# Local attention in a hybrid mixer step: four subtractions and two sums of the softmax by GpSimd, the scale of the values in ScalarE's copy

## The chip, the cores and the metric

The kernel runs on one core of a Trainium2 chip. The metric is device time in microseconds (us) of one execution. The core's engines each work through a list of their own, in order: TensorE (PE in the rows, PEld its weight loads), VectorE (DVE), ScalarE (ACT), GpSimd (POOL), and SyncE (SP), which here issues nearly all DMAs. They wait for one another by semaphores. An instruction that waits holds up everything behind it on its engine.

## The reference, cut to what matters

Two layers. In each, 2048 latent tokens (16 tiles of 128) and 128 context tokens (one tile) go through one input projection, three groups of heads (a state-space scan, gated linear attention, windowed attention) and one output projection. The change is in the windowed attention: four query heads in two key groups, 64 wide, 128 queries against up to four blocks of 128 keys, with a learned sink logit per head in the softmax and a gate on the result.

```python
qh = rms_norm(aq, q_norm); kh = rms_norm(ak, k_norm)      # per head, then rotary
s = einsum('bnqkgd,bnskd->bnkgqs', qb, k_win) * scale     # masked band, and context keys
p = softmax(concatenate([sink, s_ctx, s_loc], axis=-1))
o = einsum(p_ctx, v_ctx) + einsum(p_loc, v_win)
y_att = o * silu(ag)
```

## The kernel before

Everything is computed in float32 accuracy out of pairs of float16 numbers, an upper and a lower part: a product is three float16 matmuls (upper by lower, lower by upper, upper by upper), which is why PE has so many of them.

Each layer has a stage for attention, from about 336 to 600 us of the span in the first layer and from about 1476 to 1740 us in the second. It is a software pipeline over the 17 tiles. For a latent tile t the loop calls, in this order, `att_project` of a tile some way ahead, `att_weights` of tile t + 2, `att_values` of tile t, and `gla_out` of tile t - 1 (the end of the linear attention, which has nothing to do with the change but shares all engines). Loads of weights for the next stage (L246 to L268) lie among them.

`att_project` multiplies a tile with the weights of queries, keys and values (L281 on PE), copies queries and keys to the tile `qkx`, of which there is a single buffer (L788, L789 on ACT), squares them (L793 on GpSimd), sums the squares and adds a constant (L795, L796 on VectorE), takes the power -1/2 (L186 on GpSimd, written to `ars`), multiplies by that and by the weights of the norm (L799, L800 on VectorE), forms the rotary product (two L817 on GpSimd, L818 and L819 on VectorE), and splits the result into upper parts (L823, L722 on ACT) and lower parts (L824, L723 on VectorE). A DMA turns the parts around for PE (L828).

`att_weights` multiplies queries and keys of four heads to scores in PSUM (L854, L856), takes each head's maximum (four L857 on VectorE) and makes the negative shift `nm` of the exponential from it (L861, L864). `sd` is the sink's term: a sum of 128x4 numbers (L865, VectorE) and its exponential (L866, ACT). Then for each of the four heads: the exponential with its row sum (L872, ACT), the upper half of it (L874, ACT), the lower half, which is a subtraction of 128x512 numbers (L875: for the first head on VectorE, for the other three on GpSimd), and a DMA that turns both around (L876). At the end the row sums and the sink's term are added (L877, VectorE, 128x4), inverted (L879, VectorE), and multiplied by a scale `igv` of the values (L880, VectorE) to `rl`.

`att_values` multiplies the values with the weights (L892), copies the result out of PSUM (L895, ACT), transposes it (L898), makes the gate (L903 on ACT, L904 on VectorE), multiplies the gate by `rl` (L905, GpSimd) and both together (L907, VectorE).

The tiles `pr` and `p16`, which L872, L874 and L875 write, have two buffers each. The order of the instructions on each engine isn't that of the code: a scheduler goes over the whole program when it is built and sets it by its own estimate of costs, so an edit in one place can move instructions in others.

Of the kernel before, what the change touches and what calls it, by code (L numbers as in the profile page):

```python
# [14 lines left out]
AF = mybir.ActivationFunctionType  # L15
ALU = mybir.AluOpType
# [62 lines left out]
def hybrid_kernel(ctx, tc, a, o):  # L79
    nc = tc.nc  # L80
    V, S, G, T, D = nc.vector, nc.scalar, nc.gpsimd, nc.tensor, nc.sync
# [44 lines left out]
    def sb(tag, shape, dt=F32):  # L126
        if tag not in where:
            return small.tile(shape, dt, tag=tag, name=tag, bufs=1 if tag in ONCE else 2)
        ph, off, words, n = where[tag]
        off += words * rot(range(n), tag)  # L130
        return view(home.get(ph, work)[:, off:off + words], shape, dt)
# [699 lines left out]
    def att_blocks(s, t):  # L831
        if t == CT:
            return [(s.kt[t], s.v[t], None)]
        blocks = [(s.kct, s.vc, None)]
        if t > 0:
            blocks.append((s.kt[t - 1], s.v[t - 1], 0))
        blocks.append((s.kt[t], s.v[t], None))
        if t < NT - 1:
            blocks.append((s.kt[t + 1], s.v[t + 1], 1))
        return blocks  # L840

    def att_weights(l, s, t):

        blocks = att_blocks(s, t)
        nb = len(blocks)
        mx = sb("mx", [P, 4])
        sc = []
        for hh in range(4):
            kv, gg = hh // 2, hh % 2
            ps = psum(None, "s")  # L850
            for b, (kt, _, mk) in enumerate(blocks):
                bs = slice(b * P, (b + 1) * P)
                for j in range(2):
                    T.matmul(ps[:, bs], lhsT=s.qt[t][:, 2 * gg + kv], rhs=kt[:, 2 * kv + j], start=(j == 0), stop=(j == 1 and mk is None))  # L854
                if mk is not None:
                    T.matmul(ps[:, bs], lhsT=ident_b, rhs=amask[:, mk], start=False, stop=True)  # L856
            V.tensor_reduce(mx[:, hh:hh + 1], ps[:, :nb * P], AX.X, ALU.max)  # L857
            sc.append(ps)
            yield
        nm = sb("nm", [P, 4])  # L860
        V.scalar_tensor_tensor(nm, mx, s.isc[:, 0:1], s.sink, ALU.mult, ALU.max)  # L861

        sd = sb("sd", [P, 4])
        V.tensor_scalar(nm, nm, -1.0, 14.0 * math.log(2.0), ALU.mult, ALU.add)  # L864
        V.tensor_tensor(sd, s.sink, nm, ALU.add)  # L865
        S.activation(sd, sd, AF.Exp)  # L866
        ls = sb("ls", [P, 4])
        s.pt[t] = [view(x, [P, 2 * nb, 2, P], F16) for x in rot(s.pts, "pts")]
        for hh in range(4):
            kv, gg = hh // 2, hh % 2  # L870
            pr = sb("pr", [P, 512])[:, :nb * P]
            S.activation(pr, sc[hh][:, :nb * P], AF.Exp, scale=s.isc[:, 0:1], bias=nm[:, hh:hh + 1], accum_out=ls[:, hh:hh + 1])  # L872
            p16 = sb("p16", [P, 2, nb * P], F16)
            S.copy(p16[:, 0], pr)  # L874
            (G if hh else V).tensor_tensor(p16[:, 1], pr, p16[:, 0], ALU.subtract)  # L875
            D.dma_start_transpose(out=s.pt[t][kv][:, :, gg], in_=p16.rearrange("p j c -> p (j c)"))  # L876
        V.tensor_tensor(ls, ls, sd, ALU.add)  # L877
        s.rl[t] = rot(k_rl, "rl")
        V.reciprocal(s.rl[t], ls)  # L879
        V.tensor_scalar(s.rl[t], s.rl[t], s.igv, None, ALU.mult)  # L880

    def att_values(l, s, t):
        blocks = att_blocks(s, t)
# [2 lines left out]
        po = psum()  # L886
# [5 lines left out]
                    T.matmul(po[ks, 0:256], lhsT=blocks[b][1][:, vi, ks], rhs=pts[kv][:, pj * nb + b].rearrange("p g s -> p (g s)"), start=(n == 0), stop=(n == 3 * nb - 1))  # L892
                n += 1
        ot = sb("aoy", [P, 2, P])
        S.copy(ot, po[:, 0:256].rearrange("p (g s) -> p g s", g=2))  # L895
        py = psum()
        for gg in range(2):
            T.transpose(py[:, gg * P:(gg + 1) * P], ot[:, gg], ident)  # L898
# [561 lines left out]
```

## Time and profile before

| what | us |
|---|---|
| median of three runs | 2352.64 (2347.4 to 2353.36) |
| the profiled execution | 2334.53 |
| its span, first to last instruction | 2332.8 |
| PE busy | 2089.6 (90%) |
| VectorE busy | 1628.6 (70%) |
| ScalarE busy | 991.8 (43%) |
| GpSimd busy | 872.7 (37%) |

The profiled execution lies 18 us (0.8%) under the median of the runs and 1.7 us over its own span. A share of the whole span says little here: the stages differ, and a change in the attention stages is read from their own stretches. In a timeline row, the figure in brackets is the idle time of the engine before the instruction, and what ended it.

### The profile page before, as it was taken

How to read it: one execution, taken by the hardware profiler on the slowest of the kernel's cores; microseconds unless marked ns; L12 is line 12 of the kernel's file. 1: busy time of each engine (PE TensorE's matmuls, PEld its weight loads, DVE VectorE, ACT ScalarE, POOL GpSimd, SP SyncE). 2: the span in 40 equal slices, each digit the busy share in tenths (PEclk: the TensorE clock that was granted, in tenths of full speed). 3: DMA queues.
4: the chain of work that ended last, by engine and by line, in shares of the span. 5: the costliest groups of instructions: out<-in, count | busy, mean ns of one | idle time of the engine just before them, and what ended most of it. 6: DMA issues, size and time to landing. Idle time of an engine off the chain costs nothing. (4 is left out here: it accounts for less than half of the span.)

```text
span 2332.8 us, 53735 instructions
## 1 busy us (share of the span) xinstructions
PE 2089.6 (90%) x21245; PEld 1735.9 (74%) x21245; DVE 1628.6 (70%) x4088; ACT 991.8 (43%) x2183; POOL 872.7 (37%) x906
## 2 busy tenths in 40 slices
PE   3688958899899999899999995888999999999998
PEld 0455747778787788788888884777878778878887
DVE  2566767887789888865564656777788988864442
ACT  2443545555445334433333643555563533422221
POOL 0010014566443444544431001456643344454442
PEclk6798979999999999999999997999999999999999
DMA  8697433567611013577656123456671101265643
GB/s 294 182 256 188 108 85 87 119 150 166 135 56 37 33 42 124 164 188 177 170 151 174 42 75 93 93 110 149 154 153 55 37 32 42 78 171 167 163 141 98
DMA packets 486353, 288.02 MB, mean 123 GB/s; under 512 B 354344, under 2 KB 447924, under 8 KB 483796
## 3 DMA queue, kind: packets, MB, share of 16 engines
q1 hardware_dynamic: 483796, 271.99, 44.5%
q0 software_dynamic: 2304, 12.58, 1.6%
q8 instruction: 167, 2.74, 0.5%
q14 instruction: 86, 0.70, 0.1%
HBM read 141.11 MB, written 64.93 MB: 88 GB/s over the span
## 5 line engine op out<-in xcount | busy, mean ns | idle before, releaser
L281 PEld LDWEIGHTS <-HT 128*128 128x128 f16 x6528 | 585.3, 100 | 170.8 <-issue 93.0
L281 PE MATMUL pd<-slot,HT 128*128 128x256 f16 x3456 | 432.1, 278 | 50.0 <-ACT work L806 29.7
L281 PEld LDWEIGHTS <-slot 128*128 128x128 f16 x4320 | 394.3, 97 | 105.9 <-issue 41.2
L281 PE MATMUL pd<-slot,work 128*128 128x256 f16 x3264 | 365.5, 273 | 2.1 <-DMA work<-work 2.1
L281 PEld LDWEIGHTS <-work 128*128 128x128 f16 x3264 | 319.2, 98 | 42.6 <-DMA work<-work 2.6
L281 PE MATMUL pd<-HT,slot 128*128 128x260 f16 (+3 forms) x2592 | 316.5, 269 | 13.2 <-DMA HT<-work 12.4
L281 PE MATMUL ps<-HT,slot 128*128 128x260 f16 (+1 forms) x1728 | 201.5, 270 | 4.5 <-DVE work L1054 4.5
L281 PE MATMUL ps<-slot,HT 128*128 128x256 f16 x1440 | 175.6, 281 | 19.1 <-ACT work L1188 14.3
L1248 POOL TENSOR_TENSOR work<-work 128x512 f32<-128x512 f32 x68 | 89.2, 1312 | 185.5 <-DVE work L1247 176.3
L875 POOL TENSOR_TENSOR work<-work 128x512 f16<-128x512 f32 (+2 forms) x102 | 117.4, 1154 | 85.1 <-ACT work L874 70.3
L1054 DVE SCALAR_TENSOR_TENSOR work<-ps,work 128x256 f32<-128x256 f32 (+1 forms) x288 | 134.0, 465 | 11.9 <-ACT work L1052 7.6
L1054 DVE SCALAR_TENSOR_TENSOR work<-pd,work 128x256 f32<-128x256 f32 (+1 forms) x288 | 132.5, 464 | 3.7 <-ACT work L1052 0.9
L872 ACT ACTIVATE work<-ps,nm,K 128x512 f32<-128x512 f32 (+2 forms) x136 | 100.9, 744 | 73.1 <-DVE nm L864 58.3
L1116 POOL TENSOR_TENSOR work<-work 128x512 f32<-128x512 f32 x68 | 73.2, 1081 | 113.3 <-ACT work L1074 61.8
L1056 ACT ACTIVATE work<-work 128x256 f32<-128x256 f32 (+1 forms) x144 | 58.1, 403 | 121.0 <-DVE work L1054 82.8
L1088 POOL TENSOR_TENSOR work<-K,work 128x512 bf16<-128x512 bf16 x68 | 72.2, 1063 | 77.9 <-PE ps L1100 77.2
L281 PE MATMUL pm<-slot,HT 128*128 128x256 f16 x816 | 98.8, 277 | 1.6 <-DVE work L907 1.5
L854 PEld LDWEIGHTS <-work 128*128 128x128 f16 x1008 | 74.4, 98 | 34.7 <-issue 31.9
L874 ACT CAST work<-work 128x512 f16<-128x512 f32 (+2 forms) x136 | 78.1, 589 | 46.2 <-DMA slot<-work 26.3
L669 POOL MEMSET work<- 128x512 f32 x2 | 1.1, 525 | 256.2 <-PE pm L616 256.2
L1057 DVE SCALAR_TENSOR_TENSOR work<-work 128x256 f32<-128x256 f32 (+1 forms) x144 | 81.9, 569 | 19.1 <-ACT work L1056 18.0
L1214 ACT ACTIVATE work<-work 128x512 bf16<-128x512 f32 x68 | 42.7, 629 | 119.2 <-DMA work<-work 53.6
(374 smaller groups left out, 4035.1 us busy)
## 6 DMA issues: line engine op xcount, KB each, us to landing
slot<-in_w_in_dram SPq DMA_DIRECT2D x24, 1024.0 KB
ymix<-work SPq DMA_DIRECT2D x68, 128.0 KB
yacc<-work SPq DMA_DIRECT2D x34, 256.0 KB
work<-ymix SPq DMA_DIRECT2D x34, 256.0 KB
work<-yacc SPq DMA_DIRECT2D x34, 256.0 KB
x<-work SPq DMA_DIRECT2D x17, 512.0 KB
work<-x SPq DMA_DIRECT2D x17, 512.0 KB
out_dram<-work SPq DMA_DIRECT2D x17, 512.0 KB
```

The costliest lines, as they stand in the source:

```text
L281: T.matmul(out, lhsT=lhs(i, k), rhs=rhs(j, k), start=(n == 0), stop=(n == 3 * KB - 1))
L854: T.matmul(ps[:, bs], lhsT=s.qt[t][:, 2 * gg + kv], rhs=kt[:, 2 * kv + j], start=(j == 0), stop=(j == 1 and mk is None))
L872: S.activation(pr, sc[hh][:, :nb * P], AF.Exp, scale=s.isc[:, 0:1], bias=nm[:, hh:hh + 1], accum_out=ls[:, hh:hh + 1])
L874: S.copy(p16[:, 0], pr)
L875: (G if hh else V).tensor_tensor(p16[:, 1], pr, p16[:, 0], ALU.subtract)
L1054: V.scalar_tensor_tensor(acc[:, jj, :W], pp[:, q:q + W], s.cw[j][:, q, jj:jj + 1], acc[:, jj, :W], ALU.mult, ALU.add)
L1056: S.activation(th[:, :W], acc[:, jj, :W], AF.Tanh)
L1057: V.scalar_tensor_tensor(acc[:, jj, :W], th[:, :W], 1.0, acc[:, jj, :W], ALU.add, ALU.mult)
L1088: G.tensor_tensor(sr[:, j:j + 4], oh[:, j:j + 4].unsqueeze(2).to_broadcast([P, 4, P]), at.unsqueeze(1).to_broadcast([P, 4, P]), ALU.mult)
L1116: G.tensor_tensor(xw, x, bc8(s.wst[:, t, 8 * d:8 * d + 8]), ALU.mult)
L1214: S.activation(junk, ym[:, 512 * i:512 * i + 512], AF.Square, accum_out=ss[:, i:i + 1])
L1248: G.tensor_tensor(xs[:, js], xs[:, js], tm, ALU.add)
```

## The change

`sd` (L865) and the sum before the reciprocal (L877) go from VectorE to GpSimd. The subtraction L875 goes to GpSimd for all four heads; before, it was three of four. The multiplication by `igv` (L880) is left out, and ScalarE's copy of the values out of PSUM (L895) applies that scale instead. With 17 tiles in each of two layers, that is 34 times each.

```diff
-        V.tensor_tensor(sd, s.sink, nm, ALU.add)
+        G.tensor_tensor(sd, s.sink, nm, ALU.add)
...
-            (G if hh else V).tensor_tensor(p16[:, 1], pr, p16[:, 0], ALU.subtract)
+            G.tensor_tensor(p16[:, 1], pr, p16[:, 0], ALU.subtract)
...
-        V.tensor_tensor(ls, ls, sd, ALU.add)
+        G.tensor_tensor(ls, ls, sd, ALU.add)
         s.rl[t] = rot(k_rl, "rl")
         V.reciprocal(s.rl[t], ls)
-        V.tensor_scalar(s.rl[t], s.rl[t], s.igv, None, ALU.mult)
...
-        S.copy(ot, po[:, 0:256].rearrange("p (g s) -> p g s", g=2))
+        S.activation(ot, po[:, 0:256].rearrange("p (g s) -> p g s", g=2), AF.Copy, scale=s.igv)
```

VectorE loses 136 instructions, GpSimd gains 102, ScalarE keeps its number but for two more loads of its function table in the second layer's `ssd_decays`. Lines after L880 have a number lower by one in the changed kernel (L905 is L904 there).

The scheduler sets a new order through both attention stages and the ones that follow. On GpSimd, in the second layer, between the square of tile 10's queries and keys (L793) and the power of its sums (L186 with `ars`), this stands before:

```order
L875 TENSOR_TENSOR work<-work 128x512
L793 TENSOR_TENSOR work<-work 128x384
L875 TENSOR_TENSOR work<-work 128x512
L186 TENSOR_TENSOR ars<-avar,K 128x6
L875 TENSOR_TENSOR work<-work 128x512
L186 TENSOR_TENSOR grs<-gvar,K 128x4
L817 TENSOR_TENSOR work<-work 128x12x16 x2
```

In the changed kernel the same tile on the same engine reads:

```order
L875 TENSOR_TENSOR work<-work 128x512 x2
L793 TENSOR_TENSOR work<-work 128x384
L877 TENSOR_TENSOR ls<-ls,sd 128x4
L875 TENSOR_TENSOR work<-work 128x512
L186 TENSOR_TENSOR ars<-avar,K 128x6
L875 TENSOR_TENSOR work<-work 128x512
L186 TENSOR_TENSOR grs<-gvar,K 128x4
```

The sum L877 now stands between the two, ahead of a subtraction; it does so in 17 of 34 tiles.

On VectorE, in the second layer, tile 9, from the shift of the exponential to the lower parts of the queries and keys (L824, L723), this stands before:

```order
L864 TENSOR_SCALAR nm<-nm 128x4
L865 TENSOR_TENSOR sd<-K,nm 128x4
L904 SCALAR_TENSOR_TENSOR work<-work,pd 128x256
L818 TENSOR_TENSOR work<-work 128x384
L819 TENSOR_TENSOR work<-work 128x384
L875 TENSOR_TENSOR work<-work 128x512
L824 TENSOR_TENSOR work<-work 128x4x64
L723 TENSOR_TENSOR work<-work 128x2x128
```

In the changed kernel it is (L903 is the former L904):

```order
L864 TENSOR_SCALAR nm<-nm 128x4
L903 SCALAR_TENSOR_TENSOR work<-work,pd 128x256
L818 TENSOR_TENSOR work<-work 128x384
L819 TENSOR_TENSOR work<-work 128x384
L824 TENSOR_TENSOR work<-work 128x4x64
L723 TENSOR_TENSOR work<-work 128x2x128
```

The two rows that went to GpSimd are gone, and L824 follows L819 directly.

## Rows read from the trace of the kernel before

**Rows 1.** Busy time by stretch, both attention stages; columns in the first line.

```profile
core 0: us, PE busy (x) PEld busy (x) DVE busy (x) ACT busy (x) POOL busy (x), PEclk, DMA share, GB/s
336.00:600.00 264.00, 235.94 (x2509) 202.06 (x2506) 200.14 (x475) 148.61 (x361) 149.21 (x163) 0.98 0.59 128
...
1476.00:1740.00 264.00, 236.98 (x2582) 202.02 (x2582) 204.72 (x514) 148.99 (x360) 152.05 (x166) 0.97 0.64 139
```

**Rows 2.** Timeline, 1644.9 to 1660.8, one turn of `qkx`: start, duration, engine.

```profile
1644.99 0.47 ACT L788 ACTIVATE work<-pd,waqi 128x256 f32<-128x256 f32 x1 [0.23 <-DVE work L824]
...
1645.87 0.83 POOL L793 TENSOR_TENSOR work<-work 128x384 f32<-128x384 f32 x1 [1.25 <-ACT work L789]
...
1646.86 0.54 DVE L795 TENSOR_REDUCE avar<-work 128x6 f32<-128x384 f32 x1
...
1649.42 1.32 POOL L186 TENSOR_TENSOR ars<-avar,K 128x6 f32<-128x6 f32 x1
...
1653.95 0.55 DVE L800 TENSOR_TENSOR work<-work,K 128x384 f32<-128x384 f32 x1
...
1654.63 1.15 POOL L817 TENSOR_TENSOR work<-work 128x192 f32<-128x192 f32 x2 [1.80 <-issue]
...
1655.84 0.53 DVE L865 TENSOR_TENSOR sd<-K,nm 128x4 f32<-128x4 f32 x1
...
1656.87 0.96 DVE L819 TENSOR_TENSOR work<-work 128x384 f32<-128x384 f32 x1
...
1658.16 0.69 DVE L875 TENSOR_TENSOR work<-work 128x512 f16<-128x512 f32 x1 [0.33 <-ACT work L874]
1658.55 0.41 ACT L823 CAST work<-work 128x256 f16<-128x256 f32 x1
1658.73 1.16 POOL L875 TENSOR_TENSOR work<-work 128x512 f16<-128x512 f32 x1 [1.31 <-ACT work L874]
...
1658.99 1.18 DVE L824 TENSOR_TENSOR work<-work 128x256 f16<-128x256 f32 x1
...
1660.28 0.47 ACT L788 ACTIVATE work<-pd,waqi 128x256 f32<-128x256 f32 x1 [0.25 <-DVE work L824]
```

**Rows 3.** Groups by shape, VectorE: count, busy us, mean ns, idle before.

```profile
L875 DVE TENSOR_TENSOR work<-work 128x512 f16<-128x512 f32 x28 | 24.4, 870 | 8.4 <-ACT work L874 7.8 <-DMA work<-gen 0.5
...
L880 DVE TENSOR_SCALAR K<-K 128x4 f32<-128x4 f32 x34 | 12.2, 359 | 0.5
...
L877 DVE TENSOR_TENSOR ls<-ls,sd 128x4 f32<-128x4 f32 x34 | 9.0, 265 | 6.7 <-ACT work L872 6.6
L865 DVE TENSOR_TENSOR sd<-K,nm 128x4 f32<-128x4 f32 x34 | 8.8, 260 | 0.7
```

**Rows 4.** The same for GpSimd.

```profile
L875 POOL TENSOR_TENSOR work<-work 128x512 f16<-128x512 f32 x84 | 101.9, 1217 | 63.3 <-ACT work L874 48.8 <-issue 12.1 <-DVE K L879 0.9
...
L186 POOL TENSOR_TENSOR grs<-gvar,K 128x4 f32<-128x4 f32 x34 | 37.1, 1091 | 40.8 <-DVE gvar L698 39.7 <-DVE K L879 0.8
...
L875 POOL TENSOR_TENSOR work<-work 128x128 f16<-128x128 f32 x6 | 2.6, 442 | 10.3 <-ACT work L874 10.3
```

**Rows 5.** Line L864, VectorE: ns min/median/max.

```profile
L864 DVE TENSOR_SCALAR nm<-nm x34: 154/170/689, 338.2 to 1713.7; 128x4 f32<-128x4 f32 x34
```

**Rows 6.** Line L879, VectorE, the same columns.

```profile
L879 DVE RECIPROCAL K<-ls x34: 160/172/179, 344.7 to 1724.9; 128x4 f32<-128x4 f32 x34
```

**Rows 7.** Groups by shape, ScalarE: the exponential, the copy of the values, a table load.

```profile
L872 ACT ACTIVATE work<-ps,nm,K 128x512 f32<-128x512 f32 x112 | 86.6, 776 | 46.6 <-DVE nm L864 34.5 <-DVE work L875 7.5 <-POOL work L875 4.1
...
L895 ACT COPY work<-pm 128x256 f32<-128x256 f32 x34 | 12.8, 376 | 9.1 <-PE pm L892 9.1
...
L943 ACT ACT_TABLE_LOAD x2 | 2.6, 1283 | 0.0
```

**Rows 8.** Timeline of VectorE, 1625 to 1629, another turn of `qkx`.

```profile
1625.98 1.65 DVE L875 TENSOR_TENSOR work<-work 128x512 f16<-128x512 f32 x1
...
1627.88 0.41 DVE L824 TENSOR_TENSOR work<-work 128x256 f16<-128x256 f32 x1
```

## The prediction

> **What bounds the kernel now.** I read the busy time by stretch first, because the change touches only the two attention stages [rows 1]. Each is 264 us long, PE is busy for 236 and 237 of them, VectorE for 200 and 205, GpSimd for 149 and 152, ScalarE for 149. No engine is full, so these stages are set by waits between engines. What the stages can give at most is PE's idle time in them, 28 and 27 us, together 55 us. PE has the same matmuls to do after the change.
>
> Which waits? I followed one buffer through the timeline. The tile `qkx` exists once, so L788 can write the next tile's queries only when L824 has read the last ones. One turn is in [rows 2]: from L788 at 1644.99 to the next L788 at 1660.28, which starts 0.11 us after L824 ends (1658.99 + 1.18) and is marked as waiting for it. The turn takes 15.3 us and crosses GpSimd three times (L793, L186, L817), VectorE six times (L795, L796, L799, L800, L818 with L819, L824) and ScalarE in between. I read all 32 latent turns of the two layers in the same way: the mean from L788 to the last read is 15.3 us, and only 0.6 us more pass until the next L788. So this buffer's chain is close to the period of the stage. About 9 us of a turn are the instructions themselves. The rest is queueing: the chain's next instruction has its data, and its engine is doing something else. Summed over 32 turns that is 122 us on VectorE, 43 us on GpSimd, 26 us on ScalarE. The price of the change is what it does to these three numbers. After [rows 1] the other stages keep their work.
>
> **The change part by part.** *VectorE loses four instructions per tile.* By their busy time that is 24.4 + 12.2 + 9.0 + 8.8 = 54 us [rows 3]; this is the upper end, as if all of it lay on the path, and the lower end is 0. In the 32 turns I counted how much of each removed instruction runs while an instruction of the chain waits behind it: L875 11.2 us, L877 2.9, L865 2.0, L880 0.6, together **17 us**. [rows 8] shows the largest piece: L875 takes 1.65 us, and L824 comes only after it. In [rows 2] it is part of L865, ahead of L818 and L819. I take 17 us as the gain. The waits that go with these instructions cost VectorE another 8.4 and 6.7 us of idle time ahead of L875 and L877 [rows 3], hardly any of it ahead of the chain, so I add nothing.
>
> *GpSimd gains 34 subtractions and 68 sums of 128x4.* A subtraction is 1.22 us on average [rows 4]. A sum of 128x4 isn't in the trace on this engine. It lies between 0 and the 1.09 us of the power of 128x4 (L186), and nearer to the same kind of instruction at 128x128, 0.44 us; carrying the two sizes of L875 on in a line, (1.22 - 0.44) / 384 per number, gives about 0.2, and I estimate 0.25 us. New work on GpSimd: 34 x 1.22 + 68 x 0.25 = 58 us, 19% of its 301 us in the two stages. What of it lies on the chain depends on where it stands, and the new order tells that. Most of the added subtractions stand behind L817, where the chain has gone on to VectorE and ScalarE: they are hidden by L818 to L824 and by the next tile's L788. Between L793 and L186 of `ars`, and between that and L817, there are 60 L875 after and 56 before, and 21 sums L877. If the chain waits for all of it: 4 x 1.22 + 21 x 0.25 = 10 us. Half of what stands there is waited for today (86 us of instructions by their plain durations, 43 us of waits on this engine); the sums come first in their gaps, though, and push the rest back, so I take **7.5 us**, with 0 and 17 as ends (17 if everything that the new order has moved into these gaps, L707, L708 and other powers too, is waited for at that half and more).
>
> *The two engines disturb each other.* L864 takes 154 ns at best and 689 at worst, while L879, a reciprocal of the same size, always takes 160 to 179 [rows 5, 6]. In [rows 2] L824 takes 1.18 us and starts while GpSimd is in an L875 that ends at 1659.89; it takes 0.41 in [rows 8]. Over 32 turns such stretching of the chain's own VectorE instructions comes to 28 us. With GpSimd 19% busier in the stage I add 28 x 0.19 = **5 us**, ends 0 and 10. The Trainium skill (SBUF — State Buffer, section on the two separate sides) says of this that VectorE and GpSimd share one pair of ports, which a GpSimd instruction, or a VectorE instruction with two inputs from SBUF or in a two-port mode, holds to its end while the other is blocked; the L824 of this trace agrees, since it ends 0.28 us after the L875 beside it. By that rule the time of the four instructions isn't taken off the pair but made longer, and it is a rival below.
>
> *ScalarE.* L895 is 376 ns as a plain copy [rows 7]; L788, the same size out of PSUM with a scale, is 470 [rows 2]. So the scale costs 34 x 0.09 = 3 us on ScalarE, which is idle for 44% of the stage; the path to it goes through L892 and L898 and isn't the chain. Two more table loads are 2.6 us [rows 7], in one place, beside the same idle time. On the other side the new order has fewer exponentials L872 between L722 and the next L788, 30 instead of 39; at 0.78 us each [rows 7] that is 7 us, and by the same half as above **3 us** of gain. Ends: 7 us gain, 6 us loss.
>
> *The new waits.* L866 on ScalarE now waits for GpSimd's L865, and the remaining exponentials and L823 are queued behind it. It is covered: two L872 run between the shift and L866, and L865 stands right behind the two L817. L879 on VectorE now waits for GpSimd's L877, with L796 behind it in 14 tiles; there L877 comes directly after L793, and L795's 0.54 us cover its 0.25. If GpSimd is late there, L796 and with it the chain are late; that is in the 17 above. SP issues the four L876 one after the other, each of them held up by the pieces as they come from L875; the first head's piece now comes from the engine that makes the second, so the second is later by up to one 1.22 us, once per tile, behind which other DMAs queue. `p16` and `pr` with two buffers pass this on to L872 and L874, which are off the chain of `qkx`. I count 0 for it, with 5 us as the bad end.
>
> The sum is -17 + 7.5 + 5 - 3 = **-7.5 us**, against the profiled execution 2334.5 to 2327. That execution lies 18 us below the median; nothing says that the difference belongs to these stages, so I take the same 7.5 us off the median: 2352.6 - 7.5 = 2345.1 us, 0.3% less.
>
> **The rivals.** *GpSimd's queue takes the place of VectorE's.* The power L186 of `ars` finds L877 and an L875 ahead of it in most turns, and the chain waits for all that the new order has put there: 17 us. VectorE's relief is smaller than counted, since 6 of the 11.2 us of L875 lie ahead of L824, which can't start before ScalarE's L823 in any case: 20 - 6 = 14 us. With 5 us of stretching that gives 17 + 5 - 14 = +8, with the late DMAs +13; I take **+10 us**, 2363. It decides from the point at which the added wait on GpSimd is over 0.5 us per turn. For it: the chain passes GpSimd three times, and its instructions are longer than VectorE's. Against it: the added subtractions mostly stand behind L817.
>
> *GpSimd and VectorE stand in each other's way.* By rows: 34 x 1.22 + 68 x 0.25 on GpSimd in place of VectorE's plain 34 x 0.69 [rows 2] + 68 x 0.15 (as L864 at best [rows 5]) keeps what the two share busy for 58 - 34 = 24 us longer. If the gain is 17 and all of that lies on the path, the result is **+7 us**, 2360. It decides where chain and GpSimd meet: at L799, L800, L819 and L824. The rule of the Trainium skill named above would lead here. Against it: L879 is never stretched [rows 6], so not all of VectorE's work takes part.
>
> *The gain is given back.* The chain gets shorter, and the DMAs of the queries and keys, or PE's own order, end the next turn: **0**, 2352.6. For it speaks that the slack of 0.6 us per turn is an average, and that in about half of the turns L788 doesn't start right behind the last read.
>
> *More is gained.* What is queued behind the removed instructions off the chain (the maxima L857, the shift, L904) moves up as well, and half of VectorE's 54 us comes out: -27 + 7.5 + 5 - 3 = **-17.5 us**, 2335; with both costs at their lower end it would be -30.
>
> **How the numbers follow.** Two medians of this kernel can be told apart from about 0.3%, 7 us. Forecast (-15 to 0): 0.50, a little over half of it (0.27) above 0.3%. More gained: 0.15. Given back: 0.11. In each other's way: 0.08, of which 0.03 stay within 0.3%. GpSimd's queue: 0.16. That makes faster 0.27 + 0.15 = 0.42, same 0.23 + 0.11 + 0.03 = 0.37, slower 0.05 + 0.16 = 0.21. The range goes from -24 to +12 us, 2329 to 2364: it takes in the larger gain halfway to its good end and the queue's case almost to its bad one, and leaves out what lies beyond.
>
> **What would show it.** In the changed profile VectorE's busy time should be lower by 45 to 55 us, GpSimd's higher by about 58, with L865 and L877 at 0.2 to 0.3 us. The attention stages should be a few us shorter each, everything behind them the same length. If I am right, the turn of `qkx` falls from 15.9 to about 15.6 us, with less waiting on VectorE and a little more on GpSimd. If GpSimd's queue decides, the waits ahead of L186 and L793 grow by over 0.5 us per turn. If the two stand in each other's way, L799, L800, L819 and L824 are longer on average. What would make the prediction wrong altogether is the scheduler's order: it has changed in both stages and behind them, and a place that I did not read may gain or lose as much as the change itself.

## The result, and the profile after

The changed kernel takes 2358.91 us (median of 20 runs, 2339.48 to 2373.59), the kernel before, on the same chip, 2345.56 (median of 20, 2332.25 to 2359.16). The ratio is 1.0055, 95% interval 1.0036 to 1.0075: slower by 13 us, between 8 and 18. The forecast was 7.5 us faster. The three runs shown ahead of the prediction lay 7 us above the median of the twenty, so differences count here and not the absolute numbers. One microsecond below is 1/2346 of a ratio.

First a line of the page of the changed kernel, busy time of each engine over the whole span:

```profile
PE 2111.2 (90%) x21245; PEld 1747.1 (74%) x21245; DVE 1601.3 (68%) x3952; ACT 999.3 (42%) x2185; POOL 927.3 (39%) x1008
```


GpSimd has 55 us more, as forecast (58). VectorE has 27 us less, where 45 to 55 were forecast: half of what was taken off it is still there, in other instructions. The stretches that answer to [rows 1], with the same columns:

```profile
336.00:600.00 264.00, 234.39 (x2380) 197.17 (x2380) 182.55 (x409) 143.55 (x345) 166.57 (x204) 0.95 0.54 122
1476.00:1740.00 264.00, 237.90 (x2552) 201.47 (x2551) 188.45 (x425) 148.77 (x350) 172.21 (x209) 0.99 0.59 131
```


GpSimd rises from 149 and 152 us to 167 and 172, VectorE falls from 200 and 205 to 183 and 188, and PE does about as much in the same time. From the first L788 to the last L907 (L906 in the changed kernel), the first layer's attention stage takes 324.1 us against 315.6 in the profile before, and the second's 319.5 against 310.3. But a second profile of the kernel before (e8, below) has 321.8 and 318.3, so against that one the changed stages are only 2.3 and 1.2 us longer: two single profiles don't show where the 13 us are. What lies between the stages and behind them has its old length (791.7 and 793.0 us, 596.7 and 595.8), which was forecast. TensorE's granted clock doesn't explain the loss: averaged over the runs it is 0.949 in the changed kernel, but 0.955 in e4 and e9 (below), which lose as much, and 0.953 to 0.955 in the kernel before run beside the experiments.

GpSimd's groups in the changed kernel (count, busy us, mean ns, idle before and what ended it), which answer to [rows 4]:

```profile
L875 POOL TENSOR_TENSOR work<-work 128x512 f16<-128x512 f32 x112 | 139.7, 1255 | 51.1 <-ACT work L874 34.1 <-ACT sd L866 6.8 <-issue 5.0
...
L865 POOL TENSOR_TENSOR sd<-K,nm 128x4 f32<-128x4 f32 x34 | 8.6, 253 | 20.4 <-DVE nm L864 16.3 <-DVE wpb L196 2.8 <-DVE tcl L191 1.0
L877 POOL TENSOR_TENSOR ls<-ls,sd 128x4 f32<-128x4 f32 x34 | 7.6, 224 | 14.9 <-ACT work L872 14.3
```


The durations are those of the prediction: 1.25 us for a subtraction, 0.25 and 0.22 for a sum. What it had no term for stands behind the last bar: GpSimd is idle for 20.4 us ahead of the first sum and 14.9 ahead of the second, 35 us for 16 us of work, waiting for VectorE's shift and ScalarE's last exponential. All that time it can't begin what is queued behind.

Now one turn of `qkx` in the changed kernel's timeline (start, duration; in brackets the idle time before and its end), to be laid beside [rows 2]:

```profile
1646.10 0.47 ACT L788 ACTIVATE work<-pd,waqi 128x256 f32<-128x256 f32 x1
...
1648.84 0.82 POOL L793 TENSOR_TENSOR work<-work 128x384 f32<-128x384 f32 x1
...
1649.62 0.19 POOL L877 TENSOR_TENSOR ls<-ls,sd 128x4 f32<-128x4 f32 x1
...
1650.97 0.62 ACT L874 CAST work<-work 128x512 f16<-128x512 f32 x1 [1.76 <-DMA slot<-work]
1651.42 0.16 DVE L796 TENSOR_SCALAR avar<-avar 128x6 f32<-128x6 f32 x1
...
1651.72 1.16 POOL L875 TENSOR_TENSOR work<-work 128x512 f16<-128x512 f32 x1 [1.91 <-ACT work L874]
1652.33 0.62 ACT L874 CAST work<-work 128x512 f16<-128x512 f32 x1 [0.74 <-DMA slot<-work]
...
1653.08 1.16 POOL L875 TENSOR_TENSOR work<-work 128x512 f16<-128x512 f32 x1 [0.20 <-ACT work L874]
...
1654.20 1.32 POOL L186 TENSOR_TENSOR ars<-avar,K 128x6 f32<-128x6 f32 x1
...
1659.12 2.64 POOL L875 TENSOR_TENSOR work<-work 128x512 f16<-128x512 f32 x2
1659.28 1.12 DVE L701 TENSOR_SCALAR grs<-grs,ggh 128x4 f32<-128x4 f32 x1
...
1660.66 1.37 DVE L723 TENSOR_TENSOR work<-work 128x256 f16<-128x256 f32 x1
```


The power L186 has its data when L796 ends, at 1651.58, and starts at 1654.20, 2.6 us later. Two subtractions of 1.16 us stand ahead of it in the order. The first one waits, with GpSimd idle for 1.91 us, for ScalarE's L874, which itself waits 1.76 us until a transposing DMA has emptied its buffer; so it starts only at 1651.72, and both subtractions lie behind the end of L796. In the turn of [rows 2] one subtraction (and L905) stands in this place, and L186 starts 1.55 us after the end of its L796. In this turn the queue on GpSimd is longer than the busy times in it.

I counted all 32 latent turns as in the prediction (the chain's next instruction has its data, and its engine does something else or waits in front of something else). The kernel before was profiled a second time (e8, below), to see how far such a count moves by itself. In the table "turn" is the mean time from L788 of a latent tile to the next one, and the waits are sums over 32 turns, in us.

| kernel | ratio to before, 95% | turn | VectorE | GpSimd | ScalarE |
|---|---|---|---|---|---|
| before / the same again (e8) | 1 | 15.94 / 16.25 | 122 / 130 | 43 / 43 | 26 / 27 |
| changed | 1.0055 [1.0036, 1.0075] | 16.18 | 110 | 69 | 26 |
| e1 subtraction | 1.0029 [1.0005, 1.0053] | 16.04 | 110 | 66 | 27 |
| e3 no first subtraction | 1.0003 [0.9978, 1.0028] | 16.17 | 120 | 45 | 41 |
| e4 one subtraction more | 1.0061 [1.0042, 1.0081] | 16.32 | 128 | 51 | 32 |
| e7 other head | 0.9992 [0.9967, 1.0018] | 16.32 | 130 | 44 | 26 |
| e6 both sums | 0.9948 [0.9924, 0.9972] | 15.72 | 114 | 36 | 29 |
| e17 sum L877 | 0.9981 [0.9954, 1.0009] | 16.05 | 125 | 37 | 29 |
| e18 sum L865 | 0.9939 [0.9913, 0.9965] | 15.79 | 121 | 28 | 28 |
| e5 scale | 0.9969 [0.9946, 0.9992] | 16.01 | 125 | 44 | 30 |
| e2 sums, scale | 0.9948 [0.9924, 0.9971] | 15.86 | 119 | 44 | 26 |
| e10 subtraction, scale | 1.0014 [0.9993, 1.0034] | 16.10 | 111 | 62 | 24 |
| e9 subtraction, sums | 1.0065 [1.0040, 1.0090] | 16.28 | 115 | 67 | 26 |
| e13 subtraction, L865 | 1.0006 [0.9978, 1.0033] | 16.08 | 119 | 56 | 29 |
| e14 subtraction, L877 | 1.0053 [1.0026, 1.0081] | 15.96 | 104 | 53 | 24 |
| e11 before, second buffer | 0.9918 [0.9885, 0.9951] | 15.46 | 133 | 92 | 11 |
| e12 changed, second buffer | 0.9943 [0.9921, 0.9965] | 15.64 | 106 | 101 | 18 |
| e15 sums, scale, buffer | 0.9918 [0.9892, 0.9943] | 15.38 | 130 | 85 | 22 |
| e16 the same, `asq` twice | 0.9930 [0.9902, 0.9958] | 15.29 | 115 | 47 | 27 |

In the last four rows `qkx` has two buffers, so their waits are not comparable with those above. In the changed kernel 12 us (or 20, against the second profile) left VectorE and 26 came onto GpSimd. The moved subtraction makes that: every kernel with four subtractions on GpSimd and one buffer for `qkx` has 51 to 69 us of waits there, every one with three has 28 to 45. But these waits don't sort the times: e4 loses 14 us with 51 us of them, e10 3 us with 62, e13 1 us with 56. Nor does the turn: the changed kernel's 16.18 lies between the two of the kernel before. The lengths of both stages together (first L788 to last L907) go roughly with the times: 626 and 640 us before, 644 changed, 643 in e4, 640 in e9, 621 in e18, 617 in e6, 614 in e11; but e14, which loses 12 us, has 632.

### The profile page after: what moved, and what is told of

It reads as the page before. It is cut to its first block, busy times and chain, and to the rows that moved or that the text cites. A ratio compares the mean times of both kernels' runs of the same rounds, so it can differ in the third digit from the quotient of the medians.

```text
span 2357.2 us, 53668 instructions
## 1 busy us (share of the span) xinstructions
PE 2111.2 (90%) x21245; PEld 1747.1 (74%) x21245; DVE 1601.3 (68%) x3952; ACT 999.3 (42%) x2185; POOL 927.3 (39%) x1008
## 5 line engine op out<-in xcount | busy, mean ns | idle before, releaser
L281 PE MATMUL pd<-slot,HT 128*128 128x256 f16 x3456 | 439.0, 281 | 48.3 <-ACT work L806 30.5
L281 PEld LDWEIGHTS <-slot 128*128 128x128 f16 x4320 | 399.5, 99 | 110.5 <-issue 43.5
L875 POOL TENSOR_TENSOR work<-work 128x512 f16<-128x512 f32 (+2 forms) x136 | 159.6, 1181 | 73.6 <-ACT work L874 53.9
L874 ACT CAST work<-work 128x512 f16<-128x512 f32 (+2 forms) x136 | 78.7, 585 | 50.4 <-DMA work<-work 30.4
L857 DVE TENSOR_REDUCE mx<-ps 128x1 f32<-128x512 f32 (+2 forms) x136 | 82.1, 642 | 16.8 <-PE ps L856 14.3
L1056 DVE SCALAR_TENSOR_TENSOR work<-work 128x256 f32<-128x256 f32 (+1 forms) x144 | 79.9, 555 | 19.7 <-ACT work L1055 18.5
```

Of the source, the lines that this page charges most:

```text
L281: T.matmul(out, lhsT=lhs(i, k), rhs=rhs(j, k), start=(n == 0), stop=(n == 3 * KB - 1))
L875: G.tensor_tensor(p16[:, 1], pr, p16[:, 0], ALU.subtract)
L1056: V.scalar_tensor_tensor(acc[:, jj, :W], th[:, :W], 1.0, acc[:, jj, :W], ALU.add, ALU.mult)
```

## The experiments

Every edit lets the scheduler set a new order, so each run measures an edit together with the order that it brings. Diffs are against the kernel before, unless said otherwise; in the longer ones a line that is replaced is mostly shown in its new form alone.

**How far two profiles of one program differ.** e8 is the kernel before with an empty line more.

```diff
 LAG = 1
+
```

> The kernel before once more (one empty line more), for a second profile of it: how much the attention stages differ between two executions of the same program. Q and O both expect the same order of instructions; a difference of more than 5 us in the stages would mean that single profiles can't settle what is smaller.

One run: 2347.44 us. Its page says

```profile
span 2345.7 us, 53735 instructions
```


The profile of before had a span of 2332.8. So single profiles differ by 13 us without any edit, the turn by 0.3 us and VectorE's waits by 8, while GpSimd's waits stand at 43 in both. Spans of single profiles prove nothing here. The ratios decide; of the waits only what differs by more than these amounts can be read, such as GpSimd's.

**The parts alone.** e1 moves only the first head's subtraction.

```diff
-            (G if hh else V).tensor_tensor(p16[:, 1], pr, p16[:, 0], ALU.subtract)
+            G.tensor_tensor(p16[:, 1], pr, p16[:, 0], ALU.subtract)
```

> Only the first head's subtraction L875 goes to GpSimd; the sums and the scale stay as before. Theory Q (GpSimd's queue in the chain of qkx costs more than VectorE's relief gives): most of the loss of 13 us is here, +8 to +16 us, with the waits of the chain on GpSimd up by 20 us or more over 32 turns. Rival S (the new waits of L866 and L879 for sums on GpSimd do it): -4 to +4 us. Rival O (it is the scheduler's new order as such): any value between -10 and +15, without more waiting on GpSimd.

1.0029 [1.0005, 1.0053], 7 us slower. GpSimd has 66 us of waits instead of 43, VectorE 110. This part has the sign of the whole and about half of its size, and it was to bring most of the 17 us of gain.

e6 moves both sums and nothing else.

```diff
-        V.tensor_tensor(sd, s.sink, nm, ALU.add)
+        G.tensor_tensor(sd, s.sink, nm, ALU.add)
...
-        V.tensor_tensor(ls, ls, sd, ALU.add)
+        G.tensor_tensor(ls, ls, sd, ALU.add)
```

> Only the two sums L865 and L877 go to GpSimd. Q: VectorE loses 5 us of the chain's waits, GpSimd gains 68 short instructions; -8 to +4 us. With e5 this splits the -12 us of sums and scale. O: any value of that size, and e5 and e6 don't add up to -12.

0.9948 [0.9924, 0.9972], 12 us faster.

e5 moves only the scale.

```diff
-        V.tensor_scalar(s.rl[t], s.rl[t], s.igv, None, ALU.mult)
...
-        S.copy(ot, po[:, 0:256].rearrange("p (g s) -> p g s", g=2))
+        S.activation(ot, po[:, 0:256].rearrange("p (g s) -> p g s", g=2), AF.Copy, scale=s.igv)
```

> Only the scale moves: L880 is left out, ScalarE's copy L895 applies it. Q (GpSimd's queue in the chain of qkx decides): VectorE loses 0.6 us of the chain's waits, GpSimd nothing, so -3 to +3 us. If the 12 us that the sums and the scale together gained come from here: -6 to -15 us. Rival O (the scheduler's new order as such): any value of that size.

0.9969 [0.9946, 0.9992], 7 us faster. The copy takes 0.47 us in place of 0.38 (changed kernel: 473 ns, against 376 in [rows 7]), as forecast, and it cost nothing.

e2 has the sums and the scale, so all of the change but the subtraction.

```diff
+        G.tensor_tensor(sd, s.sink, nm, ALU.add)
...
+        G.tensor_tensor(ls, ls, sd, ALU.add)
...
-        V.tensor_scalar(s.rl[t], s.rl[t], s.igv, None, ALU.mult)
...
+        S.activation(ot, po[:, 0:256].rearrange("p (g s) -> p g s", g=2), AF.Copy, scale=s.igv)
```

> The two sums L865 and L877 on GpSimd and the scale in ScalarE's copy; the first head's subtraction stays on VectorE. Q: VectorE loses 5 us of the chain's waits and GpSimd gains little, -8 to 0 us. S: +8 to +15 us. O: any value.

0.9948 [0.9924, 0.9971], 12 us faster, no more than the sums alone: the gains do not add.

**The two halves of the moved subtraction.** e3 takes it off VectorE without giving it to GpSimd.

```diff
+        for _ in range(2):
+            V.memset(sb("p16", [P, 1024], F16), 0.0)
...
-            (G if hh else V).tensor_tensor(p16[:, 1], pr, p16[:, 0], ALU.subtract)
+            if hh:
+                G.tensor_tensor(p16[:, 1], pr, p16[:, 0], ALU.subtract)
```

> The kernel before without the first head's subtraction L875 (that head's lower half is left as the buffer holds it; two small memsets at the start of each stage). The gain alone: VectorE is freed of 34 subtractions and GpSimd gets nothing. Q: the 11 us that the chain waits behind L875 come out, -6 to -16 us. If VectorE's time isn't in the period of the stage: -3 to +3 us.

1.0003 [0.9978, 1.0028]: VectorE does less, nobody does more, and nothing is gained (between 5 us faster and 7 slower). The relief hardly reached the chain, whose waits on VectorE are 120 us, after 122 and 130. The lower parts of the queries (L824) show a part of it. Their group in the kernel before (count, busy us, mean ns, idle ahead of it):

```profile
L824 DVE TENSOR_TENSOR work<-work 128x256 f16<-128x256 f32 x34 | 20.6, 606 | 4.7 <-ACT work L823 3.9
```


in the changed kernel:

```profile
L824 DVE TENSOR_TENSOR work<-work 128x256 f16<-128x256 f32 x34 | 21.4, 628 | 16.0 <-ACT work L823 15.8
```


and in e3, where it is L826 and waits for L825:

```profile
L826 DVE TENSOR_TENSOR work<-work 128x256 f16<-128x256 f32 x34 | 22.2, 654 | 18.5 <-ACT work L825 17.2 <-DMA work<-in_const_rope_dram 1.2
```


Before, VectorE stood idle for 4.7 us ahead of L824; without the subtraction in front of it, for 16 and 18.5. It arrives earlier and waits for ScalarE's upper part. In e3 the chain's waits on ScalarE rise from 26 to 41 us, with L874 (L876 there; 9.9 to 17.8) the largest piece.

e4 leaves VectorE its work and gives GpSimd one subtraction more, whose result nobody reads.

```diff
+            if hh == 0:
+                G.tensor_tensor(view(k_hx[1], [P, nb * P], F16), pr, p16[:, 0], ALU.subtract)
```

> The kernel before with a fifth subtraction per tile on GpSimd, the first head's a second time, into a buffer that nothing reads. The cost alone: 34 more GpSimd instructions of 1.2 us, VectorE as before. Q: +12 to +30 us, since the chain waits behind them on GpSimd and VectorE keeps its queue. If GpSimd's load doesn't matter: -3 to +5 us.

1.0061 [1.0042, 1.0081], 14 us slower: this load on GpSimd alone costs as much as the whole change. The added subtraction is L877 in this kernel:

```profile
L877 POOL TENSOR_TENSOR K<-work 128x512 f16<-128x512 f32 x28 | 45.4, 1623 | 24.3 <-ACT work L874 24.2
```


It takes 1.62 us, where those of [rows 4] take 1.22, so e4 may price the moved subtraction too high. e1 has four subtractions on GpSimd as well, but also the relief, and loses 7: if the two loads cost the same, the relief is worth 7 us there, against 0 in e3. That is less than the 11.2 us counted for it in either case; these runs don't settle which.

The load shows on both engines. VectorE is busy for 1654.7 us with the instructions that take 1628.6 and 1633.2 us in the two profiles of before. Some of its groups in before:

```profile
L723 DVE TENSOR_TENSOR work<-work 128x256 f16<-128x256 f32 x36 | 18.5, 513 | 0.0
L701 DVE TENSOR_SCALAR grs<-grs,ggh 128x4 f32<-128x4 f32 x34 | 11.3, 331 | 5.2 <-POOL grs L186 5.0
```


and in e4:

```profile
L723 DVE TENSOR_TENSOR work<-work 128x256 f16<-128x256 f32 x36 | 30.1, 837 | 0.0
L824 DVE TENSOR_TENSOR work<-work 128x256 f16<-128x256 f32 x34 | 26.4, 777 | 6.0 <-ACT work L823 5.0
...
L701 DVE TENSOR_SCALAR grs<-grs,ggh 128x4 f32<-128x4 f32 x34 | 15.4, 454 | 5.2 <-POOL grs L186 5.2
```


L723 goes from 513 to 837 ns, L824 from 606 to 777. In the changed kernel it is L723 and L701:

```profile
L723 DVE TENSOR_TENSOR work<-work 128x256 f16<-128x256 f32 x36 | 25.9, 720 | 0.0
...
L701 DVE TENSOR_SCALAR grs<-grs,ggh 128x4 f32<-128x4 f32 x34 | 18.4, 540 | 10.2 <-POOL grs L186 10.0
```


e7 gives VectorE the fourth head's subtraction in place of the first's: as much work on each engine, another order.

```diff
-            (G if hh else V).tensor_tensor(p16[:, 1], pr, p16[:, 0], ALU.subtract)
+            (V if hh == 3 else G).tensor_tensor(p16[:, 1], pr, p16[:, 0], ALU.subtract)
```

> The same work on each engine as before, but VectorE takes the subtraction L875 of the fourth head and GpSimd those of the first three. Nothing moves between engines, so only the order and the place differ. O: it shows how much a new order alone is worth, up to 10 us either way. Q: GpSimd then has the first two heads' pieces in a row, behind L817; 0 to +8 us.

0.9992 [0.9967, 1.0018]: no difference clear of the noise (8 us faster to 4 slower). This one new order does not make 13 us; others could.

**Do the parts add?** By the parts alone, subtraction and sums would give 7 - 12 = -5 us. e9 has both.

```diff
+            G.tensor_tensor(p16[:, 1], pr, p16[:, 0], ALU.subtract)
...
+        G.tensor_tensor(sd, s.sink, nm, ALU.add)
...
+        G.tensor_tensor(ls, ls, sd, ALU.add)
```

> The subtraction and the two sums go to GpSimd; the scale stays on VectorE's reciprocals. Apart, the subtraction cost 7 us and the sums gained 12; if each keeps its price, -5 us. Theory X (what is short on GpSimd is worth its move only while the subtractions leave room; with four of them the sums stand behind them and L879 on VectorE waits): +5 to +15 us, as the whole change. Then the scale has no part in the loss.

1.0065 [1.0040, 1.0090], 15 us slower. The sums, worth 12 us with three subtractions on GpSimd, cost 8 with four. The intervals of e1 and e9 overlap a little, but the product of e1 and e6, 0.998, lies far below that of e9.

e10 has subtraction and scale.

```diff
+            G.tensor_tensor(p16[:, 1], pr, p16[:, 0], ALU.subtract)
...
-        V.tensor_scalar(s.rl[t], s.rl[t], s.igv, None, ALU.mult)
...
+        S.activation(ot, po[:, 0:256].rearrange("p (g s) -> p g s", g=2), AF.Copy, scale=s.igv)
```

> The subtraction goes to GpSimd and the scale to ScalarE; the sums stay on VectorE. If each keeps its price, 7 - 7 = 0 us (-4 to +4). Theory X says the same, since the sums aren't moved. If it is +8 us or more, the scale's gain goes with the subtraction's move too, and the loss isn't in the sums.

1.0014 [0.9993, 1.0034], 3 us slower: 7 by the subtraction, 4 given back by the scale. Here the parts nearly add, so it is the sums that do not get on with the fourth subtraction.

Which sum? e13 has the subtraction and L865, e14 the subtraction and L877.

```diff
+            G.tensor_tensor(p16[:, 1], pr, p16[:, 0], ALU.subtract)
...
+        G.tensor_tensor(sd, s.sink, nm, ALU.add)
```

> The subtraction and the sum of the sink L865 go to GpSimd, L877 and the scale stay. In the changed kernel GpSimd stands idle 16 us ahead of L865 for VectorE's L864 and 14 us ahead of L877 for ScalarE's L872, with subtractions queued behind. Theory W (the sums cost by their waits in GpSimd's own order, once four subtractions stand behind them): half of the 8 us by which the sums made the subtraction's move worse, so about +11 us; if L865's wait is the one that counts, +15. If the sums keep the price that they had alone, about +1 us.

1.0006 [0.9978, 1.0033], 1 us: L865 takes 5 us off the subtraction.

```diff
+            G.tensor_tensor(p16[:, 1], pr, p16[:, 0], ALU.subtract)
...
+        G.tensor_tensor(ls, ls, sd, ALU.add)
```

> The subtraction and the sum L877 go to GpSimd, L865 and the scale stay. W: the other half, about +11 us; if L877's wait is the one that counts, +15 us. If the sums keep the price that they had alone, about +1 us.

1.0053 [1.0026, 1.0081], 12 us slower: L877 adds 5 to it. Either difference to e1 is smaller than the intervals can tell; the intervals of e13 and e14, 11 us apart, overlap only a little.

Each sum alone, with three subtractions on GpSimd:

```diff
-        V.tensor_tensor(ls, ls, sd, ALU.add)
+        G.tensor_tensor(ls, ls, sd, ALU.add)
```

> Of the change only one sum: L877 (row sums and sink's term, 128x4) on GpSimd; L865 and the first head's subtraction stay on VectorE. The two sums together gave 12 us less than before. Theory 'L877 is harmful wherever it stands, because GpSimd waits in it for ScalarE's last exponential': 0 to +5 us against before, and the wait of L877 for L872 on GpSimd near the 8 us that it had in the kernel with L877 and four subtractions. Theory 'L877 is harmful only behind a fourth subtraction, because GpSimd is then later with everything': -4 to -8 us, about half of the 12.

0.9981 [0.9954, 1.0009], -4 us, from -11 to +2.

```diff
-        V.tensor_tensor(sd, s.sink, nm, ALU.add)
+        G.tensor_tensor(sd, s.sink, nm, ALU.add)
```

> Of the change only the other sum: L865 (sink's term, 128x4) on GpSimd. By the first theory (L877 harmful anywhere) all of the 12 us that both sums gave come from here: -9 to -15 us. By the second (both help while GpSimd has three subtractions) about half: -4 to -8 us, as L865 took 7 us off when it was added to the four subtractions.

0.9939 [0.9913, 0.9965], 14 us faster, as much as both sums: by these values L865 brings the gain, and L877 adds nothing to it.

GpSimd's groups in e18, with the columns of above:

```profile
L875 POOL TENSOR_TENSOR work<-work 128x512 f16<-128x512 f32 x84 | 104.5, 1248 | 45.7 <-ACT work L874 31.8 <-issue 8.9 <-POOL work L707 1.6
...
L865 POOL TENSOR_TENSOR sd<-K,nm 128x4 f32<-128x4 f32 x34 | 9.9, 292 | 9.4 <-DVE nm L864 8.8
```


and in e13, where only the fourth subtraction has been added:

```profile
L875 POOL TENSOR_TENSOR work<-work 128x512 f16<-128x512 f32 x112 | 135.9, 1220 | 48.6 <-ACT work L874 40.7 <-ACT sd L866 6.7 <-DVE work L693 0.5
...
L865 POOL TENSOR_TENSOR sd<-K,nm 128x4 f32<-128x4 f32 x34 | 9.3, 274 | 21.0 <-DVE nm L864 17.3 <-DVE gvar L698 3.1
```


The same sum of 0.3 us holds GpSimd idle for 9.4 us in the one and 21.0 in the other. The order puts it in another place, and GpSimd's chain waits are 28 and 56 us. That alone doesn't price it: beside the subtraction, with 21.0 us of idle time, L865 still takes 5 us off e1. For L877 there is no such difference: it waits 9.1 us in e17 and 8.1 in e14, and e14 has the lowest VectorE waits of all and a turn of 15.96. Whether it really costs 5 us beside four subtractions, and why, is **open**.

**Does the loss go through the turn of `qkx`?** e11 is the kernel before with a second buffer for it, in a tile that lies idle in this stage.

```diff
-        x = sb("qkx", [P, 6, 64])
+        x = view(k_hx[1], [P, 6, 64]) if t % 2 else sb("qkx", [P, 6, 64])
```

> The kernel before with a second buffer for qkx, every other tile in memory that is idle in this stage; no work is moved. If the turn of qkx is the period of the stage, the next tile's L788 can start before L824 is done, and the stages get shorter: -10 to -30 us. If another buffer or PE's order holds the next tile anyway: -5 to +5 us.

0.9918 [0.9885, 0.9951], 19 us faster. The single buffer was a bound of the stage. Its windows of the two stages, with the columns of [rows 1]:

```profile
336.00:600.00 264.00, 235.77 (x2478) 200.62 (x2478) 209.41 (x502) 149.23 (x362) 152.91 (x164) 0.97 0.59 129
1476.00:1740.00 264.00, 240.36 (x2654) 206.26 (x2652) 204.38 (x520) 156.15 (x368) 156.95 (x169) 0.99 0.66 141
```


In the second layer PE is busy for 3.4 us more of the same stretch than in [rows 1], with 72 matmuls more; in the first this profile shows no difference. From the first L788 to the last L907 the stages take 311.1 and 302.6 us, both shorter than in either profile of the kernel before. e12 has the same buffer in the changed kernel (the other lines are those of the change).

```diff
-        x = sb("qkx", [P, 6, 64])
+        x = view(k_hx[1], [P, 6, 64]) if t % 2 else sb("qkx", [P, 6, 64])
```

> The changed kernel with the second buffer for qkx. If the loss of the change comes through the turn of qkx, it goes away with the second buffer: within 5 us of e11. If GpSimd's load costs by another way (the pieces for the DMAs, the sums ahead of L879), the difference of about 13 us to e11 remains.

0.9943 [0.9921, 0.9965], 13 us faster than before, 6 slower than e11. By these values about half of the loss of 13 us is left when the turn is no bound any more. But the intervals of e11 and e12 overlap: run against run, e12 lies between 2 us under e11 and 13 over it. That a part of the loss goes through the turn is likely by this, and not shown.

e15 adds sums and scale to e11.

```diff
-        x = sb("qkx", [P, 6, 64])
+        x = view(k_hx[1], [P, 6, 64]) if t % 2 else sb("qkx", [P, 6, 64])
...
+        G.tensor_tensor(sd, s.sink, nm, ALU.add)
...
+        G.tensor_tensor(ls, ls, sd, ALU.add)
...
-        V.tensor_scalar(s.rl[t], s.rl[t], s.igv, None, ALU.mult)
...
+        S.activation(ot, po[:, 0:256].rearrange("p (g s) -> p g s", g=2), AF.Copy, scale=s.igv)
```

> The two sums on GpSimd, the scale on ScalarE, the subtraction on VectorE, and the second buffer for qkx: the two changes that gained, together. If they add up, 12 + 19 = -31 us. If the turn of qkx was the way by which the sums gained, hardly more than the second buffer alone: -19 to -24 us.

0.9918 [0.9892, 0.9943], 19 us faster (13 to 25), the same as e11: with a second buffer the sums and the scale don't bring their 12 us on top, which would have made 31. So the turn is the likely way by which they gained.

e16 doubles the next single tile of the chain, `asq`, as well.

```diff
+        x = view(k_hx[1], [P, 6, 64]) if t % 2 else sb("qkx", [P, 6, 64])
...
+        sq = view(k_hx[0], [P, 6, 64]) if t % 2 else sb("asq", [P, 6, 64])
...
+            r = view(k_hx[0], [P, 6, 64]) if t % 2 else sb("asq", [P, 6, 64])
...
+        G.tensor_tensor(sd, s.sink, nm, ALU.add)
...
+        G.tensor_tensor(ls, ls, sd, ALU.add)
...
-        V.tensor_scalar(s.rl[t], s.rl[t], s.igv, None, ALU.mult)
...
+        S.activation(ot, po[:, 0:256].rearrange("p (g s) -> p g s", g=2), AF.Copy, scale=s.igv)
```

> As e15, and the tile of the squares and of the rotary product (asq) gets a second buffer as well. With qkx twice, L793 waits 2.3 us per turn, since asq exists once and is read last by L819. If that is the next bound, 5 to 15 us under e15; if PE or the DMAs are, within 4 us of e15.

0.9930 [0.9902, 0.9958], 16 us faster, no more than e15. The wait ahead of L793 falls from 1.93 to 1.03 us per turn and nothing comes of it, so this tile is not the next bound.

e11 and e15 beat the kernel before by 19 us and the changed one by 32; e18, one line, beats before by 14.

## Why the prediction was wrong, point by point

**The bound was read rightly.** The turn of `qkx` sets much of the attention stages: e11 gains 19 us, and stays under the 55 us that [rows 1] left as the most. That everything behind keeps its length held too.

**The gain of 17 us was not there.** This is the step that failed, with its largest term, the 11.2 us of L875. "In the 32 turns I counted how much of each removed instruction runs while an instruction of the chain waits behind it" counts time that is taken from a queue, and not time by which the chain ends sooner. e3 takes the largest piece off and gains 0 (at best 5); by e4 against e1 the same relief is worth 7, if their loads cost the same. Part of the time went into the next thing that L824 needs (idle ahead of it 4.7 to 16.0 and 18.5 us), and on VectorE other rows of the queue moved up: in the changed kernel the chain waits 10.6 us behind a weight copy (L258), which was 3.7. My rival had put 6 of these 11.2 us down to L823 and kept the rest. The two sums are missed the other way: the count gave them 2.9 and 2.0, and moving them gains 12 us (e6), L865 alone 14 (e18). So the count misses in both directions; it leaves out where the new order puts everything else, which I take for the reason and no run shows by itself.

**The 7.5 us on GpSimd were mis-sized.** e4 prices the subtraction's load alone at 14 us, and in the changed kernel the chain's waits on GpSimd rose by 26 us, of which VectorE's gave back 12 to 20. "Half of what stands there is waited for today" was taken of plain durations, 1.22 and 0.25 us, and both durations were right. But GpSimd waits in front of an L875 for ScalarE, which waits in L874 for a DMA, and all of that stands ahead of L186. Between the end of the chain's last step and its next one on GpSimd, L875 accounts for 33.3 us (before 19.3), other powers L186 for 8.1 (0.0), L708 for 4.7 (1.4), and idle time ahead of such instructions for 7.4 (4.2).

**The waits of the sums themselves were not priced at all.** "The new waits" followed L866 and L879, which wait for the sums, and found them covered. The sums wait too: 35 us of idle GpSimd in the changed kernel, 18 in e6. On VectorE the same two waited for 7.4 us [rows 3]. What this idle time costs is **open**: with 17.5 us of it e6 gains 12, with 21.0 e13 is level with the kernel before, with 35 the changed kernel loses 13.

**The stretching was seen, and about right on the chain.** Forecast were 5 us on the chain, ends 0 and 10. To its last read, which is L723, the chain's own VectorE instructions went from 4.02 to 4.27 us per turn, 8 us in 32; nearly all of that is L723, and with L824 as the last it is 1 us (4.12 to 4.15). L723 frees the keys' part of `qkx` for L789, and ScalarE's idle time ahead of L789 for this reason goes from 0.7 to 2.9 us, in e4 to 5.0. Off the chain there is more of it: e4 has, with unchanged VectorE work, 21 to 26 us more busy time. In the changed kernel's turn above, L723 takes 1.37 us beside the second of two L875 that end at 1661.76, and ends 0.27 us after it; L701, which treats 128x4 numbers, takes 1.12 us beside the first. The Trainium skill (SBUF — State Buffer, section on the two separate sides) would have it so: one of the two engines holds the shared pair for a whole instruction and the other is blocked. This trace agrees. How much of the loss the rival that this rule leads to carries isn't shown, since no run has the load without the stretching. Its named marks were the wrong ones: L799, L800, L819 and L824 grew by 3 to 6% (732 to 759 ns, 648 to 665, 622 to 658, 606 to 628), and L723 and L701 by 40 and 63%.

**ScalarE.** The 3 us of gain did not show: the chain's waits there are 26 us as before. The price of the scale was right per instruction, and the sign of the edit was wrong, since e5 gains 7 us (2 to 13). Taking L880, 12.2 us, off VectorE was worth more than the count's 0.6; whether by its own time or by the order that came with it, these runs don't separate.

**SP's late pieces** were counted at 0. SP's queue, waiting for subtractions before it issues a transposing DMA (us in total, times, longest), in the kernel before:

```profile
SPq L876 <- POOL work L875: 31.2, 29, 3.0
SPq L876 <- DVE work L875: 5.9, 6, 1.7
```


and in the changed kernel, where all subtractions are GpSimd's:

```profile
SPq L876 <- POOL work L875: 69.9, 41, 5.3
```


ScalarE's exponentials, waiting for the subtraction to free their buffer, in the kernel before:

```profile
ACT work L872 <- DVE work L875: 8.8, 13, 1.8
ACT work L872 <- POOL work L875: 5.4, 7, 1.9
```


and in the changed kernel:

```profile
ACT work L872 <- POOL work L875: 14.0, 21, 1.5
```


So SP's wait goes from 37 to 70 us, and ScalarE's stays at 14: what it waited for on VectorE it now waits for on GpSimd. Does SP's longer wait cost time? Hardly by itself: it is 58 us in e7 and 72 in e13, which take as long as the kernel before. Where the 6 us come from that e12 is over e11, if they are real, is **open**; no run took `p16` or `pr` by itself.

**The rivals.** "GpSimd's queue takes the place of VectorE's" came nearest: +10 against 13 (8 to 18), and its mark was met, since the waits ahead of L793 and L186 went from 0.44 + 0.66 to 0.69 + 1.02 us per turn, 0.6 more where 0.5 was the point. Its working was less good, so that it came so near is partly luck: it still had 14 us of relief on VectorE, and in e4, which loses as much, the same two waits are only 0.16 us per turn longer. What the runs put in place of the sum: moving the subtraction costs 7 us net (e1), with a load of up to 14 (e4) against a relief of 0 to 7; the sums, which gain 12 us by themselves (e6), cost 8 beside it (e9). Whether the load costs by the queue, the stretching or the buffers is not separated.

## What to carry to other kernels

Before work is moved to an engine that is half idle, look at what its queue waits for and not only at how long it is busy: an added instruction brings its own wait into an in-order queue. One run that adds the load without the relief, and one that gives the relief without the load, price the two halves for a few lines of edit, as far as the halves add. Time freed ahead of a chain's instruction counts only if its other inputs are there. And where one buffer's turn is the bound, a second buffer (19 us here) can be worth as much as the best move of work between the engines of the turn (14 us, e18), and it moves no work.

## What the runs showed of the hardware

- A sum of 128x4 on GpSimd takes 0.19 us at best and 0.20 in the median (changed kernel), where a power of 128x4 takes 1.01. On VectorE the same sum was 0.26 on average [rows 3] and 0.16 in the median, so at this size GpSimd is hardly slower.
- The subtraction of 128x512 takes 1.16 us on GpSimd against 0.69 on VectorE [rows 2], 1.7 times. The Trainium skill (GPSIMD Engine Reference, 3.1) has 1.96 times for a sum of 2048 columns; no run here has that size.
- Twenty runs of one program spread over 27 us (2332 to 2359), and VectorE's busy time in two profiles of it differs by 5 us, GpSimd's by 0.4.
- One more subtraction per tile on GpSimd makes VectorE's unchanged instructions 21 to 26 us longer in all (e4), and adds 56 us to GpSimd's own busy time, 51 of them by the 34 subtractions themselves.
